# Wide and narrow products in turn: a tuned float32 trunk kernel with another order of its matmuls behind the mixer

## The chip, the cores and the metric

The kernel runs on one core of one Trainium2 chip. The metric is the device time of one execution in microseconds, lower being better. Profiles come from the hardware profiler; names such as L394 are lines of the kernel, PE is the matmul engine, DVE and ACT are the vector and the scalar engine, SP issues most of the transfers.

## The reference, cut to what matters

Two layers, each a token mixer and a gated feed-forward, run over 256 tokens of width 2048 in float32. Nearly all the work is products with large weights: `w_in` and `w_out` of both mixers, `w_up` (2048 by 11264) and `w_down` (5632 by 2048) of both feed-forwards.

```
for i in range(DEPTH):                      # DEPTH = 2
    h = rms_norm(x, mix_norm_w[i])
    x = x + (ssd_mixer(h, ...) if i == 0 else short_conv_mixer(h, ...))
    h = rms_norm(x, ffn_norm_w[i])
    x = x + conv_ffn(h, ffn_w_up[i], ffn_conv_w[i], ffn_conv_b[i], ffn_w_down[i])
return rms_norm(x, final_norm_w)

def short_conv_mixer(u, w_in, conv_w, w_out):
    bg, cg, h = jnp.split(u @ w_in, 3, axis=-1)
    return (bg * causal_dwconv(cg * h, conv_w)) @ w_out

def conv_ffn(u, w_up, conv_w, conv_b, w_down):
    hu = causal_dwconv(u @ w_up, conv_w, conv_b)
    g, v = jnp.split(hu, 2, axis=-1)
    return (jax.nn.silu(g) * v) @ w_down
```

## The kernel before, in words

Each float32 product is made of faster ones. A weight `w` is split on the chip into a rounded high part `wh` (a cast on ACT, L305) and the rest `wl` (a subtraction on DVE, L306); activations are kept as pairs of such parts side by side in one tile `hl`, 256 columns high part and 256 columns low part. Two products then do: a **wide** one, `wh` against all 512 columns, and a **narrow** one, `wl` against the 256 columns of the high part. A wide and a narrow product with the same block of weights are called a pair here.

Weights come in **units**: 256 rows by 512 columns, 512 KB, loaded by SP in the order of a plan, cast and split, with four buffers of `wh` and `wl`. A **stream** is one group of 512 output columns: it runs over all its units and sums into two PSUM tiles (`main`, made of two output blocks each). A unit holds two row blocks `k` and four column blocks `t`, so it gives eight pairs. A stream with 16 row blocks has 64 pairs, the down products of the first feed-forward have 24 row blocks in its first part (96 pairs) and 20 in the second (80 pairs).

Behind the first mixer all streams but those of the second down product go through `late_stream`. It works a unit in two halves of four pairs: half 0 fills the first PSUM tile, half 1, one unit behind, the second. The order of the matmuls on PE is fixed by `follow`, which chains each matmul to the one before it; the scheduler places everything else (DVE, ACT, small matmuls of a norm, recorded at L211 and L204, and the transposes at L906) by its own estimate of times. What `size` says sets the order inside a half: `size` wide products, then the `size` narrow ones of the same blocks.

- `size` 1 (streams with 16 row blocks): wide, narrow, wide, narrow.
- `size` 2 (the down streams): two wide, two narrow. "Two and two" below.
- `size` 4: in every stream, for the last two halves of the second PSUM tile. "Four and four" below.

The streams in order, with names that the text uses: the first feed-forward has part 1 (6 chunks, for each a gate stream and a value stream, then 4 down streams) and part 2 (5 chunks, then 4 down streams); then the second mixer, 12 streams `in` and 4 streams `out`; then the second feed-forward, part 1 (6 chunks) and part 2 (5 chunks), whose down products use another loop (L946 to L948, three wide products each).

When a PSUM tile is complete, `evac` reads it: ACT copies the columns 256 to 511 (L412), DVE adds the others (L414) and scales, convolves and gates.

Of the kernel before, what the change touches and what calls it, by code (L numbers as in the profile page):

```python
# [16 lines left out]
P = 128  # L17
T = 256
D = 2048
NKD = D // P  # L20
# [10 lines left out]
DFF = 5632  # L31
EPS = 1e-5
KU = 2
COLS = 512
WB = 4
FPARTS = ((0, 24), (24, 44))
ALL_COLS = tuple((cg, 0, DFF // P) for cg in range(D // COLS))
# [4 lines left out]
def trunk_kernel(ctx, tc, a, out):  # L42
# [20 lines left out]
    def follow(inst):  # L63

        if last_main[0] is not None:
            tc.add_manual_dep(
                inst.ins, last_main[0],
                mybir.DependencyInfo(
                    mybir.DependencyClass.NoSync, mybir.DependencyReason.DATA
                ),  # L70
                reason="stream order",
            )
        last_main[0] = inst.ins.name
        return inst
# [3 lines left out]
    def uid(s):  # L78
        n_id[0] += 1
        return f"{s}_{n_id[0]}"  # L80
# [61 lines left out]
    for name, r in rows:  # L142
        base[name] = at
        lo = 0
        while lo < r.shape[0]:
            i, off = divmod(at, P)
            n = min(P - off, r.shape[0] - lo)
# [72 lines left out]
    def rep2(t):  # L220
        return t.unsqueeze(1).to_broadcast([P, 2, T])

    def new_hl(pool=None):
        return (pool or hlpool).tile([P, 2, 2 * T], F32R, tag="hl", name=uid("hl"))
# [91 lines left out]
    def weight_unit(c0, kc, ahead=WB - 1):  # L316

        i = taken[0]
        assert plan[i][1:] == (c0, kc), (plan[i], c0, kc)
        taken[0] += 1  # L320
        while len(units) < min(i + ahead + 1, len(plan)):
            load_unit()
        got, units[i] = units[i], None
        return got
# [46 lines left out]
        for p in range(2):  # L371
            evac(p, pts[p])

    def late_stream(c0, hls, kcs, evac):


        pts = [psm.tile([P, 2, 512], F32, tag="main", name=uid("main")) for _ in range(2)]
        n = len(kcs)
        held = {}

        def half(p, u):
            wh, wl = held[u]
            blocks = [(t, k) for t in (2 * p, 2 * p + 1) for k in range(KU)]
            if p == 1 and u + 2 * KU >= n:
                size = len(blocks)
            else:
                size = 1 if n == NKD else KU
            for b in range(0, len(blocks), size):
                for w in (wh, wl):
                    for t, k in blocks[b : b + size]:  # L390
                        i = u + k
                        hl = hls[i // 2][:, i % 2, :]
                        cols = slice(0, 2 * T if w is wh else T)
                        follow(mm(  # L394
                            pts[p][:, t % 2, cols], w[:, k, t * P : (t + 1) * P], hl[:, cols],
                            start=(i == 0 and w is wh), stop=(i == n - 1 and w is wl),
                        ))

        for u in range(0, n + KU, KU):
            if u < n:  # L400
                held[u] = weight_unit(c0, kcs[u], WB - 2)
                half(0, u)
            if u:
                half(1, u - KU)
            while len(units) < min(taken[0] + WB - 1, len(plan)):
                load_unit()
        for p in range(2):
            evac(p, pts[p])
# [60 lines left out]
    xp, xhl = [], []  # L469
# [294 lines left out]
            hls.append(h)  # L764
        return hls

    def residual_stream(hls, kcs, norm, nhl, nname, put=stream, parts=ALL_COLS):

        if norm is not None:
            nhl += [None] * (NKD // 2)
        left = {cg: len(kcs) for cg, _, _ in parts}
        for cg, lo, hi in parts:
            hi = min(hi, len(kcs))
            left[cg] -= hi - lo

            def evac(p, pt, cg=cg, final=(left[cg] == 0)):
                m = 2 * cg + p  # L780
                x = xp[m]
                tt(out=x, in0=pt[:, :, 0:T], in1=x, op=ALU.add)
                tt(out=x, in0=pt[:, :, T : 2 * T], in1=x, op=ALU.add)
                if norm is not None and final:
                    norm.add(x)
                    h = new_hl()
                    split_pair(h, x, *nname(m))
                    nhl[m] = h

            put(cg * COLS, hls[lo // 2 : hi // 2], kcs[lo:hi], evac)  # L790

    yhl = []
    norm = Norm()
    nhl = []
# [33 lines left out]
    def ffn_part(l, part, hls, r):  # L828
        lo, hi = FPARTS[part]
        res = []  # L830
        for ch in range(lo, hi, 4):
            gs = []

            def evac_g(p, pt, ch=ch):
                k0 = ch + 2 * p
                y = conv(scaled(pt, r), W_FF, f"fw{l}", NF, k0, f"fb{l}", "g", gpool)
                act(y, y, AF.Silu)
                gs.append(y)

            def evac_v(p, pt, ch=ch):  # L840
                k0 = DFF // P + ch + 2 * p
                y = conv(scaled(pt, r), W_FF, f"fw{l}", NF, k0, f"fb{l}")
                tt(out=y, in0=gs[p], in1=y, op=ALU.mult)
                h = new_hl(hlpool2 if len(res) < 4 else hlpool)
                split_pair(h, y)
                res.append(h)

            late_stream(ch * P, hls, range(NKD), evac_g)
            late_stream(DFF + ch * P, hls, range(NKD), evac_v)
        return res  # L850

    xhl, nhl = nhl, []
    r = norm.row()
    norm = Norm()
# [9 lines left out]
    xhl, nhl = nhl, []  # L864
    r = norm.row()
    norm = Norm()
# [3 lines left out]
    for i in range(D // COLS):  # L870
        vs = [None, None]

        def evac_c(p, pt):
            s = pair_sum(pt)
            tt(out=s, in0=s, in1=rep2(r2), op=ALU.mult)
            vs[p] = s

        def evac_h(p, pt):
            s = pair_sum(pt)
            tt(out=s, in0=s, in1=vs[p], op=ALU.mult)  # L880
            vs[p] = conv(s, W_SC, "scw", NKD, 4 * i + 2 * p)

        def evac_b(p, pt):
            s = scaled(pt, r)
            tt(out=s, in0=s, in1=vs[p], op=ALU.mult)
            h = new_hl()
            split_pair(h, s)
            yhl.append(h)

        for n, ev in ((1, evac_c), (2, evac_h), (0, evac_b)):  # L890
            late_stream(n * D + i * COLS, xhl, range(NKD), ev)
    residual_stream(
        yhl, range(NKD), norm, nhl, lambda m: ("ffn", NKD + 2 * m), late_stream
    )
# [2 lines left out]
    xhl = nhl  # L897
# [30 lines left out]
    for part in range(2):  # L928
        lo, hi = FPARTS[part]
        hid = ffn_part(1, part, xhl, r)  # L930
        n = hi - lo
        for cg in range(D // COLS):
# [17 lines left out]
            def evac(c):  # L950
                x = xtok[c][:, cols]
                tt(out=x, in0=pt[:, c, :], in1=x, op=ALU.add)  # L952
                if part == 1:
                    junk = tmp.tile([P, 512], F32, tag="tp", name=uid("tp"))
                    act(junk, x, AF.Square, accum_out=ss[:, c, cg : cg + 1])
                    tt(out=x, in0=x, in1=fin[:, cols], op=ALU.mult)
                if end:
                    finish(c)
# [42 lines left out]
```

## Time and profile before

| what | value |
| --- | --- |
| median of 3 runs | 2541.95 us (2540.92 to 2543.9) |
| profiled execution, its time | 2543.58 us |
| its span, first to last instruction | 2541.7 us |
| PE busy | 2521.4 us (99%) |
| PE weight loads (beside PE's products) | 2194.3 us (86%) |
| DVE busy | 1782.5 us (70%) |
| ACT busy | 1356.2 us (53%) |
| transfers | 478.65 MB, mean 188 GB/s |
| granted TensorE clock | 0.999 |

A matmul's row in a timeline gives the start and a modelled duration. Durations overlap, since products are pipelined, so the pace is read from start to start. `x4` in such a row means four equal instructions in a run, merged into one line.

### The profile page before, as it was taken

What the parts mean: (1) busy time and instruction counts of PE and PEld (TensorE: products, weight loads), DVE (VectorE), ACT (ScalarE), POOL (GpSimd) and SP (SyncE); (2) the same over time, 40 slices, a digit from 0 to 9 for tenths busy, and PEclk for the clock granted to TensorE, in tenths of its full rate; (3) what the DMA queues carried; (4) which work ended last, traced back from release to release, by engine and by line L of the source; (5) the groups of instructions that cost most, each with busy time, mean ns of one, the idle gap of its engine ahead of it and who ended that gap; (6) DMA issues with size and microseconds to landing.
All of it is one profiled execution on the core that took longest, in us unless ns stands there. A gap on an engine that the chain in (4) does not pass through costs nothing.

```text
span 2541.7 us, 36880 instructions
## 1 busy us (share of the span) xinstructions
PE 2521.4 (99%) x14397; PEld 2194.3 (86%) x14397; DVE 1782.5 (70%) x2467; ACT 1356.2 (53%) x1738; POOL 1.1 (0%) x8
## 2 busy tenths in 40 slices
PE   9999999999999999999999999999999999999998
PEld 8888888888888888888888888888888888888886
DVE  7788875788777776557776666666677764577764
ACT  5676654566555554345554444444555553455543
POOL 0000000000000000000000000000000000000000
PEclk9999999999999999999999999999999999999999
DMA  7566656665666666666666666666566666666664
GB/s 229 176 192 197 190 179 190 190 174 177 200 182 191 191 190 187 188 190 190 191 191 187 186 190 190 189 189 193 174 188 189 189 198 191 190 185 190 190 198 141
DMA packets 255728, 478.65 MB, mean 188 GB/s; under 512 B 17667, under 2 KB 29123, under 8 KB 255427
## 3 DMA queue, kind: packets, MB, share of 16 engines
q1 hardware_dynamic: 254643, 474.13, 62.0%
q8 instruction: 112, 1.84, 0.3%
q10 hardware_dynamic: 912, 2.18, 0.2%
q14 instruction: 61, 0.50, 0.1%
HBM read 474.09 MB, written 2.16 MB: 187 GB/s over the span
## 4 chain that ended last, share of the span: by engine, by line
PE 98%; DMA 1%; DVE 1%; ACT 0%; issue 0%; SPq 0%; ACTq 0%; DVEq 0%
PE main L394 62%; PE main L360 15%; PE main L343 8%; PE main L946 3%; PE main L947 3%; PE main L948 3%; PE aux L725 1%; DMA raw<-in_ssd_w_in_dram 1%; DMA cbc<-cs_d 0%; PE aux L733 0%; PE aux L706 0%; PE aux L579 0%; PE aux L204 0%; PE main L358 0%; DVE wl L306 0%
## 5 line engine op out<-in xcount | busy, mean ns | idle before, releaser
L306 DVE TENSOR_TENSOR wl<-raw,wh 128x1024 fp32r<-128x1024 f32 (+1 forms) x881 | 1076.0, 1222 | 703.2 <-ACT wh L305 691.9
L394 PE MATMUL main<-hl,wh 128*128 128x512 f32 x4544 | 1516.0, 392 | 0.0
L305 ACT CAST wh<-raw 128x1024 fp32r<-128x1024 f32 (+1 forms) x881 | 924.6, 1050 | 1063.8 <-PE main L394 604.8
L394 PE MATMUL main<-hl,wl 128*128 128x256 f32 x4544 | 1154.2, 280 | 0.0
L394 PEld LDWEIGHTS main<-hl,wh 128*128 128x128 f32 x4544 | 818.7, 187 | 151.0
L394 PEld LDWEIGHTS main<-hl,wl 128*128 128x128 f32 x4544 | 838.6, 189 | 39.6
L360 PE MATMUL main<-hl,wh 128*128 128x512 f32 x1728 | 542.5, 397 | 1.4 <-DVE tp L420 1.3
L343 PEld LDWEIGHTS main<-hl,wl 128*128 128x128 f32 x1792 | 331.4, 188 | 76.2 <-DVE wl L306 3.5
L343 PE MATMUL main<-hl,wl 128*128 128x256 f32 x1792 | 359.2, 280 | 2.2 <-DVE wl L306 2.2
L360 PEld LDWEIGHTS main<-hl,wh 128*128 128x128 f32 x1728 | 266.5, 189 | 8.1 <-issue 4.9
L946 PE MATMUL main<-wh,hl 128*128 128x512 f32 x352 | 137.4, 390 | 0.8 <-DVE xtok L952 0.8
L947 PE MATMUL main<-wl,hl 128*128 128x512 f32 x352 | 137.5, 391 | 0.0
L948 PE MATMUL main<-wh,hl 128*128 128x512 f32 x352 | 137.0, 389 | 0.0
L412 ACT COPY tp<-main 128x512 f32<-128x512 f32 x150 | 86.7, 578 | 31.3 <-PE main L394 24.5
L414 DVE TENSOR_TENSOR tp<-main,tp 128x512 f32<-128x512 f32 x150 | 102.5, 683 | 0.6 <-ACT tp L412 0.6
L436 DVE SCALAR_TENSOR_TENSOR tp<-tp,prm,tp 128x255 f32<-128x255 f32 x208 | 90.3, 477 | 0.0
L423 DVE TENSOR_TENSOR tp<-tp,rrow 128x512 f32<-128x512 f32 x118 | 81.2, 688 | 1.9
L946 PEld LDWEIGHTS main<-wh,hl 128*128 128x128 f32 x352 | 66.1, 188 | 15.4 <-DVE xtok L952 1.2
L948 PEld LDWEIGHTS main<-wh,hl 128*128 128x128 f32 x352 | 66.1, 188 | 14.0
L947 PEld LDWEIGHTS main<-wl,hl 128*128 128x128 f32 x352 | 66.1, 188 | 13.6
L436 DVE SCALAR_TENSOR_TENSOR g<-tp,prm,g 128x254 f32<-128x254 f32 (+1 forms) x176 | 75.0, 477 | 1.2 <-ACT g L434 1.2
L434 ACT ACTIVATE tp<-tp,prm,prm 128x256 f32<-128x256 f32 x88 | 48.0, 593 | 1.6 <-DVE tp L423 1.6
(140 smaller groups left out, 1011.7 us busy)
## 6 DMA issues: line engine op xcount, KB each, us to landing
raw<-in_ffn_w_up_dram SPq DMA_DIRECT2D x352, 512.0 KB, 4.0
raw<-in_ffn_w_down_dram SPq DMA_DIRECT2D x176, 512.0 KB, 3.7
raw<-in_ssd_w_in_dram SPq DMA_DIRECT2D x159, 512.0 KB, 4.7
raw<-in_sc_w_in_dram SPq DMA_DIRECT2D x96, 512.0 KB, 3.8
raw<-in_ssd_w_out_dram SPq DMA_DIRECT2D x64, 512.0 KB, 3.8
raw<-in_sc_w_out_dram SPq DMA_DIRECT2D x32, 512.0 KB, 3.7
cbc<-cs_d SPq DMA_DIRECT2D x32, 256.0 KB, 5.8
xt<-in_x_dram SPq DMA_DIRECT2D x8, 256.0 KB, 6.8
```

Of the source, the lines that this page charges most:

```text
L305: put(nc.scalar.copy(wh[:, ks, :], raw[:, ks, :]))
L306: put(tt(out=wl[:, ks, :], in0=raw[:, ks, :], in1=wh[:, ks, :].bitcast(F32), op=ALU.subtract,))
L343: put(mm(pts[t // 2][:, t % 2, 0:T], wl[:, k, t * P : (t + 1) * P], hls[i // 2][:, i % 2, 0:T], start=False, stop=(i == n - 1),))
L360: put(mm(o, wh[:, k, lw], hl, start=first, stop=False))
L394: follow(mm(pts[p][:, t % 2, cols], w[:, k, t * P : (t + 1) * P], hl[:, cols], start=(i == 0 and w is wh), stop=(i == n - 1 and w is wl),))
L412: nc.scalar.copy(pb, pt[:, :, T : 2 * T])
L414: tt(out=s, in0=pt[:, :, 0:T], in1=pb, op=ALU.add)
L423: tt(out=s, in0=s, in1=rep2(r), op=ALU.mult)
L436: stt(out=y[:, j, d:T], in0=s[:, j, 0 : T - d], scalar=pcol(wname, (width - 1 - d) * nk + k0 + j), in1=y[:, j, d:T], op0=ALU.mult, op1=ALU ...
L946: follow(mm(pt[:, c, :], hi_, wh[:, k, :], start=(i == 0), stop=False))
L947: follow(mm(pt[:, c, :], hi_, wl[:, k, :], start=False, stop=False))
L948: follow(mm(pt[:, c, :], lo_, wh[:, k, :], start=False, stop=(i == n - 1)))
```

## The change

In `late_stream`, `size` is now 1 everywhere, also in the down streams and in the last halves of a stream. Only where a stream is called with `settle=True` does it run two and two, and its last two halves of the second PSUM tile four and four. Settled are:

- the first gate stream of each part of both feed-forwards (`ch == lo`),
- the first value stream of the second feed-forward (`ch == 0 and l == 1`),
- the first `in` stream of the second mixer (`i == 0 and n == 1`),
- the last column block of the first feed-forward's down product, in each part (2 streams).

That is six streams with 16 row blocks, which were alternating before, and two down streams, which stay as they were.

```
-            if p == 1 and u + 2 * KU >= n:
-                size = len(blocks)
-            else:
-                size = 1 if n == NKD else KU
+            size = 1
+            if settle:
+                size = len(blocks) if p == 1 and u + 2 * KU >= n else KU
...
-            put(cg * COLS, hls[lo // 2 : hi // 2], kcs[lo:hi], evac)
+            if put is late_stream and len(kcs) != NKD and cg == D // COLS - 1:
+                kw = {"settle": True}
+            put(cg * COLS, hls[lo // 2 : hi // 2], kcs[lo:hi], evac, **kw)
...
-            late_stream(ch * P, hls, range(NKD), evac_g)
-            late_stream(DFF + ch * P, hls, range(NKD), evac_v)
+            late_stream(ch * P, hls, range(NKD), evac_g, ch == lo)
+            late_stream(DFF + ch * P, hls, range(NKD), evac_v, ch == 0 and l == 1)
...
-            late_stream(n * D + i * COLS, xhl, range(NKD), ev)
+            late_stream(n * D + i * COLS, xhl, range(NKD), ev, i == 0 and n == 1)
```

No instruction is added or taken away on any engine. SP and POOL keep their order row for row; PE, DVE and ACT change theirs from the first feed-forward on. The built programs show it at three places; line numbers of the changed kernel are three to five higher (L397 is the old L394).

On PE, the end of the first gate stream of the first feed-forward (a settled one) and the start of the next. `main_7101` and `main_7102` are its PSUM tiles, `main_7305` the next stream's first. Before:

```order
L204 MATMUL aux_7095<-dg_7092,ones 128x128 x2
L394 MATMUL main_7101<-hl_7056,wh_7201 128x512
L394 MATMUL main_7101<-hl_7056,wl_7202 128x256
L394 MATMUL main_7101<-hl_7056,wh_7201 128x512
L394 MATMUL main_7101<-hl_7056,wl_7202 128x256
L394 MATMUL main_7102<-hl_7046,wh_7179 128x512 x4
L394 MATMUL main_7102<-hl_7046,wl_7180 128x256 x4
L394 MATMUL main_7102<-hl_7056,wh_7201 128x512 x4
L394 MATMUL main_7102<-hl_7056,wl_7202 128x256 x4
L394 MATMUL main_7305<-hl_6848,wh_7223 128x512
L394 MATMUL main_7305<-hl_6848,wl_7224 128x256
```

The same place in the changed kernel:

```order
L397 MATMUL main_7101<-hl_7056,wh_7201 128x512 x2
L397 MATMUL main_7101<-hl_7056,wl_7202 128x256 x2
L397 MATMUL main_7101<-hl_7056,wh_7201 128x512
L204 MATMUL aux_7095<-dg_7092,ones 128x128 x2
L397 MATMUL main_7101<-hl_7056,wh_7201 128x512
L397 MATMUL main_7101<-hl_7056,wl_7202 128x256 x2
L397 MATMUL main_7102<-hl_7046,wh_7179 128x512 x4
L397 MATMUL main_7102<-hl_7046,wl_7180 128x256 x4
L397 MATMUL main_7102<-hl_7056,wh_7201 128x512 x4
L397 MATMUL main_7102<-hl_7056,wl_7202 128x256 x4
L397 MATMUL main_7305<-hl_6848,wh_7223 128x512
L397 MATMUL main_7305<-hl_6848,wl_7224 128x256
```

The body went from alternating to two and two, the end stays four and four, and the norm's small matmuls (L204) moved by one product.

On PE, the end of the next stream, the first value stream (`main_7305`, `main_7306`), and the start of the one behind it (`main_7515`). Before:

```order
L394 MATMUL main_7305<-hl_7056,wl_7406 128x256
L394 MATMUL main_7306<-hl_7046,wh_7383 128x512 x4
L394 MATMUL main_7306<-hl_7046,wl_7384 128x256 x4
L394 MATMUL main_7306<-hl_7056,wh_7405 128x512 x4
L394 MATMUL main_7306<-hl_7056,wl_7406 128x256 x4
L394 MATMUL main_7515<-hl_6848,wh_7427 128x512
L394 MATMUL main_7515<-hl_6848,wl_7428 128x256
```

In the changed kernel:

```order
L397 MATMUL main_7306<-hl_7056,wh_7405 128x512
L397 MATMUL main_7306<-hl_7056,wl_7406 128x256
L397 MATMUL main_7515<-hl_6848,wh_7427 128x512
L397 MATMUL main_7515<-hl_6848,wl_7428 128x256
L397 MATMUL main_7515<-hl_6848,wh_7427 128x512
```

The four and four at the end is gone: the products alternate through the end of the stream and into the next.

On DVE, the eviction of that value stream (`main_7306`) among the splits of the next weights. Before:

```order
L306 TENSOR_TENSOR wl_7472<-raw_7469,wh_7471 128x1024
L306 TENSOR_TENSOR wl_7528<-raw_7525,wh_7527 128x1024
L436 SCALAR_TENSOR_TENSOR tp_7488<-tp_7485,prm_127,tp_7488 128x255 x2
L414 TENSOR_TENSOR tp_7501<-main_7306,tp_7499 128x512
L436 SCALAR_TENSOR_TENSOR tp_7488<-tp_7485,prm_126,tp_7488 128x254 x2
L423 TENSOR_TENSOR tp_7501<-tp_7501,rrow_7098 128x512
```

In the changed kernel (L439, L417, L426 and L848 are the old L436, L414, L423 and L843):

```order
L306 TENSOR_TENSOR wl_7472<-raw_7469,wh_7471 128x1024
L439 SCALAR_TENSOR_TENSOR tp_7488<-tp_7485,prm_127,tp_7488 128x255 x2
L439 SCALAR_TENSOR_TENSOR tp_7488<-tp_7485,prm_126,tp_7488 128x254 x2
L306 TENSOR_TENSOR wl_7528<-raw_7525,wh_7527 128x1024
L417 TENSOR_TENSOR tp_7501<-main_7306,tp_7499 128x512
L848 TENSOR_TENSOR tp_7488<-g_7284,tp_7488 128x512
L426 TENSOR_TENSOR tp_7501<-tp_7501,rrow_7098 128x512
```

One split (`wl_7528`) moved behind four passes of the convolution; ACT moves the cast that belongs to it behind two activations.

More of the change, by code (lines that the diff above doesn't have):

```diff
@@ L372, in stream, with late_stream @@
             evac(p, pts[p])
-    def late_stream(c0, hls, kcs, evac):
+    def late_stream(c0, hls, kcs, evac, settle=False):
         pts = [psm.tile([P, 2, 512], F32, tag="main", name=uid("main")) for _ in range(2)]
@@ L765, in ssd_gate, with residual_stream @@
         return hls
-    def residual_stream(hls, kcs, norm, nhl, nname, put=stream, parts=ALL_COLS):
+    def residual_stream(hls, kcs, norm, nhl, nname, put=stream, parts=ALL_COLS, **kw):
         if norm is not None:
```

## Prediction

> **What bounds the kernel now.** First the page: busy times, the chain that ended last, the costliest groups.
>
> ```profile
> PE 2521.4 (99%) x14397; PEld 2194.3 (86%) x14397; DVE 1782.5 (70%) x2467; ACT 1356.2 (53%) x1738; POOL 1.1 (0%) x8
> ...
> PE 98%; DMA 1%; DVE 1%; ACT 0%; issue 0%; SPq 0%; ACTq 0%; DVEq 0%
> ...
> L306 DVE TENSOR_TENSOR wl<-raw,wh 128x1024 fp32r<-128x1024 f32 (+1 forms) x881 | 1076.0, 1222 | 703.2 <-ACT wh L305 691.9
> L394 PE MATMUL main<-hl,wh 128*128 128x512 f32 x4544 | 1516.0, 392 | 0.0
> L305 ACT CAST wh<-raw 128x1024 fp32r<-128x1024 f32 (+1 forms) x881 | 924.6, 1050 | 1063.8 <-PE main L394 604.8
> L394 PE MATMUL main<-hl,wl 128*128 128x256 f32 x4544 | 1154.2, 280 | 0.0
> ```
>
> PE carries 98% of the chain, and behind the 4544 wide and 4544 narrow products of `late_stream` stands no idle time at all. So a reordering can only act through the pace from one product's start to the next, or by making PE wait where it doesn't now. Second, who waits for whom, over all engines:
>
> ```profile
> DVE wl L306 <- ACT wh L305: 691.9, 540, 4.1
> ACT wh L305 <- PE main L394: 604.8, 493, 3.5
> ```
>
> The columns are total us, times, longest. DVE waits for casts, and casts wait for PE to give up a weight buffer: the supply of weights runs as far ahead as four buffers let it. PE is the bound, not DVE (70%), ACT (53%) or the transfers.
>
> Third, the timeline of PE, for the pace. A value stream in part 2 of the first feed-forward, up to its end:
>
> ```profile
> 1172.16 0.40 PE L394 MATMUL main<-hl,wh 128*128 128x512 f32 x1
> ...
> 1172.86 0.39 PE L394 MATMUL main<-hl,wh 128*128 128x512 f32 x1
> 1173.09 0.28 PE L394 MATMUL main<-hl,wl 128*128 128x256 f32 x1
> ...
> 1190.54 0.39 PE L394 MATMUL main<-hl,wh 128*128 128x512 f32 x1
> ...
> 1191.58 1.09 PE L394 MATMUL main<-hl,wh 128*128 128x512 f32 x4
> 1192.50 0.64 PE L394 MATMUL main<-hl,wl 128*128 128x256 f32 x4
> 1192.98 1.09 PE L394 MATMUL main<-hl,wh 128*128 128x512 f32 x4
> 1193.91 0.63 PE L394 MATMUL main<-hl,wl 128*128 128x256 f32 x4
> 1194.38 0.40 PE L394 MATMUL main<-hl,wh 128*128 128x512 f32 x1
> ```
>
> Between the wide products at 1172.86 and 1190.54 lie 51 alternating pairs: 17.68 us, **346.7 ns a pair**. The eight pairs done four and four take 1191.58 to 1194.38, 2.80 us, **350 ns a pair**. Two and two, in the second down stream of part 1 (20 groups of two pairs):
>
> ```profile
> 1021.22 0.63 PE L394 MATMUL main<-hl,wh 128*128 128x512 f32 x2
> ...
> 1035.15 0.63 PE L394 MATMUL main<-hl,wh 128*128 128x512 f32 x2
> ```
>
> 13.93 us over 40 pairs: **348.2 ns**. But alternating has a second pace. The last part of the second feed-forward begins behind the other loop's products:
>
> ```profile
> 2197.69 0.39 PE L948 MATMUL main<-wh,hl 128*128 128x512 f32 x1
> 2197.91 0.39 PE L394 MATMUL main<-hl,wh 128*128 128x512 f32 x1
> ...
> 2198.97 0.40 PE L394 MATMUL main<-hl,wh 128*128 128x512 f32 x1
> ...
> 2216.99 0.40 PE L394 MATMUL main<-hl,wh 128*128 128x512 f32 x1
> ```
>
> 2198.97 to 2216.99 is again 51 pairs, 18.02 us: **353.3 ns**. Same instructions, same clock, 6.6 ns a pair slower, and it holds for a whole stream and the next. The instructions of L394 by stretch tell the two apart by the middle one of the three wide durations (least, median, most), 391 ns fast and 398 ns slow:
>
> ```profile
> L394 PE MATMUL main<-hl,wh x640: 387/391/398, 727.4 to 948.8; 128*128 128x512 f32 x160
> ...
> L394 PE MATMUL main<-hl,wh x128: 389/398/403, 2197.9 to 2242.4; 128*128 128x512 f32 x128
> ...
> L394 PE MATMUL main<-hl,wh x64: 389/398/477, 703.9 to 726.6; 128*128 128x512 f32 x64
> ...
> L394 PE MATMUL main<-hl,wh x65: 389/396/476, 1819.1 to 1844.7; 128*128 128x512 f32 x65
> ...
> L394 PE MATMUL main<-hl,wh x64: 387/391/397, 1439.1 to 1461.6; 128*128 128x512 f32 x64
> ```
>
> Ten streams from 727.4 are fast; slow are the first gate stream (703.9, behind the mixer's loop), the first value stream of the second feed-forward (1819.1, most of it, with transposes between) and the two at 2197.9. So the pace depends on what stood ahead, it persists, and the four and four at a stream's end is where it turns from slow to fast (727.4, 2243) or doesn't (between the two at the end).
>
> Last, the lengths of whole streams, from the first wide product of one to that of the next (columns: stretch, length, PE, weight loads, DVE, ACT, POOL, clock, transfers):
>
> ```profile
> 1172.16:1194.38 22.22, 22.22 (x130) 19.57 (x129) 15.34 (x21) 12.63 (x17) 0.00 (x0) 1.00 0.66 190
> 1005.20:1038.64 33.44, 33.44 (x195) 29.24 (x194) 17.10 (x17) 12.61 (x13) 0.00 (x0) 1.00 0.62 189
> 1355.56:1383.42 27.86, 27.86 (x162) 24.37 (x161) 16.83 (x20) 13.15 (x17) 0.00 (x0) 1.00 0.62 189
> 2197.91:2220.49 22.58, 22.58 (x129) 19.60 (x128) 11.56 (x12) 9.27 (x10) 0.00 (x0) 1.00 0.60 170
> 2220.49:2243.07 22.58, 22.58 (x130) 19.62 (x129) 15.35 (x21) 12.62 (x17) 0.00 (x0) 1.00 0.62 186
> 703.89:727.35 23.46, 23.46 (x138) 20.52 (x137) 17.69 (x35) 12.35 (x17) 0.00 (x0) 1.00 0.59 168
> 1439.14:1462.29 23.15, 23.15 (x138) 20.48 (x137) 17.71 (x35) 11.93 (x17) 0.00 (x0) 1.00 0.60 183
> 1819.14:1844.69 25.55, 25.55 (x158) 22.59 (x157) 15.36 (x21) 15.54 (x23) 0.00 (x0) 1.00 0.53 155
> ```
>
> **The change part by part.** A fully alternating stream of 16 row blocks at the fast pace takes 64 x 346.7 = 22.19 us; of 24 row blocks 96 x 346.7 = 33.28, of 20 row blocks 27.73. A settled stream of 16 takes 56 x 348.2 + 8 x 350 = 22.30.
>
> 1. Four and four taken out of streams that alternate. Behind the mixer stand 60 streams of 16 row blocks; 6 are settled, one more (2220.49) was slow, 53 remain: 22.22 - 22.19 = 0.033 us each, unrounded. Gain 1.75 us.
> 2. The stream at 2220.49, no longer behind a slow one: 22.58 - 22.19. Gain 0.39 us.
> 3. Down streams, three in each part, from two and two to alternating: 3 x (33.44 - 33.28) + 3 x (27.86 - 27.73). Gain 0.87 us.
> 4. The six settled ones. The norm's small products cost 23.15 - 22.22 = 0.93 us in a stream. First gate stream: 22.30 + 0.93 = 23.23 for 23.46, gain 0.23. Part 2 of the first feed-forward, the second mixer's first stream and the first gate stream of the second feed-forward were fast: a loss of 0.08 each, 0.24. The value stream at 1819.14 was slow for more than half its 64 pairs, 32 to 64 x 6.6 ns = 0.2 to 0.4, less 0.08: gain 0.1 to 0.3, taken as 0.15. The stream at 2197.91: 22.58 - 22.30 = 0.28. Together a gain of 0.42.
> 5. What the scheduler moved. DVE is busy for at most 17.7 of 23 us in any of the streams above, so the split that goes behind four passes has 5 us of slack a stream; the norm's products come, by the built order, twelve products (some 2 us) earlier in one stream and later in another. Taken as nothing: DVE's idle time and the buffers ahead cover it. If that cover were gone, the next half of PE would start late, by about the 1050 ns of one cast (L305).
> 6. Buffers and PSUM tiles of a stream's end are given up later, by three narrow products: at 0.64 us for four (the row at 1192.50) less than 0.5 us, behind the same cover.
>
> Sum 1.75 + 0.39 + 0.87 + 0.42 = **3.4 us** gained, against the profiled execution's span of 2541.7: 2538.3. That execution took 2543.58 us, 1.63 above the median of 2541.95, so the forecast in the metric is 2541.95 - 3.4 = **2538.6 us**.
>
> All this holds only if alternation runs at the fast pace. Before, it was set anew at the end of each stream; now it runs on from a settled stream to the next settled one, in five stretches: 11 streams and 3 down streams (992 pairs), 9 and 3 (816), 15 of the second mixer (960), 10 (640) and 9 (576). The price of a slow stretch is its pairs times 6.6 ns: 6.6, 5.4, 6.4, 4.3 and 3.8 us, 26 us for all. What the trace has of the way into a stretch: two and two all through, then four and four, then alternating, as here behind the last down stream of part 1:
>
> ```profile
> 1104.10 1.09 PE L394 MATMUL main<-hl,wh 128*128 128x512 f32 x4
> 1105.03 0.63 PE L394 MATMUL main<-hl,wl 128*128 128x256 f32 x4
> 1105.50 0.40 PE L394 MATMUL main<-hl,wh 128*128 128x512 f32 x1
> ...
> 1106.55 0.39 PE L394 MATMUL main<-hl,wh 128*128 128x512 f32 x1
> ```
>
> Three pairs in 1.05 us, fast. The stream at 1439.1 (391 ns) entered in the same way. Two of two, but both behind down streams without a small matmul inside. Behind the mixer's two and two without a four and four, alternation was slow (703.9). I take the fast pace for each stretch, by the two nearest rows, with doubt for each; the second stretch most, whose first stream is now settled directly behind another settled one, which no row shows. How alternation goes over the down streams' own activation tiles no row shows either: between 346.7 and 353.3 ns.
>
> **The rivals.**
> - One stretch falls into the slow pace and keeps it: 2538.6 + 3.8 to 6.6 = 2542.4 to 2545.2; with the second, 2544.0. For it: the slow pace went through one stream's end into the next at 2220.49. Against: of the four slow streams three ended fast, and all streams begun fast and left undisturbed stayed so; but there are no such ends now to mend a slow one.
> - Two or more stretches slow, the case on the other side: from 2538.6 + 3.8 + 4.3 = 2546.7 up to 2565 with all five. It decides from about 1300 slow pairs (8.5 us, by which the gain is lost and 0.2% more).
> - The order makes no difference, so that nothing is gained: 2542. Four paces for the same work in the rows above speak against it. The Trainium skill (TensorE: Matmul & The Clock Gate, section "Back-to-back issue gap") gives a product alone N / 2.4 + 2.5 ns; as an estimate that is 215.8 + 109.2 = 325 ns a pair in any order. By that rule the sum is zero; the trace does not agree, with 346.7 to 353.3 by order and history.
> - Late weights: a cast or split comes late in each of the 54 alternating streams. At 1050 ns each that is 57 us; the waits above speak against it.
>
> **How the numbers follow.** This measurement tells about 0.2%, 5.1 us, from no change. Fast throughout 47%, 2537.5 to 2539.5; one slow stretch 30%; two or more 13%; no difference 4%; late weights 2%; a gain past 5.1 us, by a pace that no row shows or in the measurement, 4%. The first, second and fourth lie within 0.2% but for a little noise: faster 5%, same 80%, slower 15%. The range takes in the fast case with its noise and one slow stretch: 2536.5 to 2546.5.
>
> **What the profile after would show.** PE's groups of `late_stream` still without idle time; streams of 22.19 us, the down streams 33.28 and 27.73 but for the last, 22.3 for settled ones, and a median wide duration of 391 ns in all five stretches. A stretch of 22.6 us streams with 398 ns would show the first rival, waits of PE for L306's successor the last. What makes me wrong is mainly a state that I can read but not derive.

## The result, and the profile after

The changed kernel takes 2548.95 us (median of 9 runs, 2547.67 to 2551.55), the one before 2541.95 (median of 9, 2539.42 to 2543.9): a ratio of 1.003, with a 95% interval of 1.0021 to 1.0039. It is slower by 7 us, where the forecast said faster by 3.4 and allowed up to 2546.5. The profiled execution took 2551.55 us, with a span of 2549.3, which is 7.6 above the span before.

First the page of the changed kernel: busy times, chain, costliest groups (L397 is the old L394).

```profile
PE 2529.3 (99%) x14397; PEld 2196.0 (86%) x14397; DVE 1789.4 (70%) x2467; ACT 1355.7 (53%) x1738; POOL 1.1 (0%) x8
...
PE 98%; DMA 1%; DVE 1%; ACT 0%; issue 0%; SPq 0%; DVEq 0%; ACTq 0%
...
L306 DVE TENSOR_TENSOR wl<-raw,wh 128x1024 fp32r<-128x1024 f32 (+1 forms) x881 | 1075.6, 1222 | 700.4 <-ACT wh L305 692.2
L397 PE MATMUL main<-hl,wh 128*128 128x512 f32 x4544 | 1566.2, 394 | 0.0
L305 ACT CAST wh<-raw 128x1024 fp32r<-128x1024 f32 (+1 forms) x881 | 923.8, 1049 | 1053.9 <-PE main L397 638.5
L397 PE MATMUL main<-hl,wl 128*128 128x256 f32 x4544 | 1225.8, 280 | 0.0
```

PE is the bound as before, and behind its products of `late_stream` still stands no idle time (the last column is 0.0). The two groups of products show 1566 and 1226 us of busy time, more than before, but these sums overlap and are not lengths. Who waits for whom, over all engines (total us, times, longest):

```profile
DVE wl L306 <- ACT wh L305: 692.2, 584, 4.1
ACT wh L305 <- PE main L397: 638.5, 466, 3.4
```

Casts wait for PE 34 us longer in all: the supply of weights has more slack, not less. So nothing came late. The loss is in PE's pace, and the windows show where. Each row is one stretch between two first wide products, with the late products alone (columns: window, length, PE, weight loads, clock, transfers). The rows are the 11 up streams of stretch 1, its three alternating down streams, the 9 up streams of stretch 2, its three down streams, the 15 of the second mixer, the first 9 of stretch 4, the first 8 of stretch 5. Before:

```profile
727.35:971.77 244.42, 244.42 (x1410) 215.27 (x1409) 1.00 0.64 189
971.77:1072.07 100.30, 100.30 (x579) 87.69 (x577) 1.00 0.61 189
1127.72:1327.70 199.98, 199.98 (x1154) 176.13 (x1153) 1.00 0.65 190
1327.70:1411.28 83.58, 83.58 (x482) 73.10 (x481) 1.00 0.62 189
1462.30:1795.60 333.30, 333.30 (x1923) 293.55 (x1922) 1.00 0.63 189
1844.69:2044.67 199.98, 199.98 (x1154) 176.13 (x1153) 1.00 0.65 190
2220.49:2398.61 178.12, 178.12 (x1026) 156.62 (x1025) 1.00 0.64 189
```

After:

```profile
726.68:970.74 244.06, 244.06 (x1410) 215.19 (x1409) 1.00 0.64 189
970.74:1072.40 101.66, 101.66 (x579) 88.27 (x578) 1.00 0.61 187
1128.15:1331.67 203.52, 203.52 (x1154) 176.59 (x1153) 1.00 0.64 187
1331.67:1416.33 84.66, 84.66 (x482) 73.57 (x481) 1.00 0.61 186
1467.42:1800.22 332.80, 332.80 (x1922) 293.43 (x1921) 1.00 0.63 189
1849.32:2052.84 203.52, 203.52 (x1155) 176.40 (x1153) 1.00 0.64 186
2228.75:2406.25 177.50, 177.50 (x1027) 156.50 (x1025) 1.00 0.65 190
```

Stretches 1, 3 and 5 gained 0.36, 0.50 and 0.62 us. Stretches 2 and 4 lost 3.54 each (some 3.9 with the tenth stream of stretch 4), and the two groups of down streams lost 1.36 and 1.08. In stretch 2 every stream takes 203.52 / 9 = 22.61 us, 353.3 ns a pair: the slow pace that the prediction had read, kept for nine streams. The late products' wide durations (least, median, most) in that stretch say the same, 398 in the middle:

```profile
L397 PE MATMUL main<-hl,wh x576: 395/398/403, 1128.2 to 1331.3; 128*128 128x512 f32 x192
```

Two places are to be explained: how a stretch gets its pace, and why the down streams have the slow one though stretch 1 ran into them at the fast one. First the way into stretch 1 (fast) and into stretch 2 (slow), from PE's timeline (start, modelled duration, run length at the end of the row). Both come out of a settled gate stream through the same two halves of four and four; the one into stretch 1 has the norm's small products three products ahead of them.

```profile
723.90 1.08 PE L397 MATMUL main<-hl,wh 128*128 128x512 f32 x4
724.81 0.64 PE L397 MATMUL main<-hl,wl 128*128 128x256 f32 x4
725.28 1.09 PE L397 MATMUL main<-hl,wh 128*128 128x512 f32 x4
726.22 0.63 PE L397 MATMUL main<-hl,wl 128*128 128x256 f32 x4
726.68 0.40 PE L397 MATMUL main<-hl,wh 128*128 128x512 f32 x1
...
727.73 0.39 PE L397 MATMUL main<-hl,wh 128*128 128x512 f32 x1
```

```profile
1125.34 1.09 PE L397 MATMUL main<-hl,wh 128*128 128x512 f32 x4
1126.27 0.63 PE L397 MATMUL main<-hl,wl 128*128 128x256 f32 x4
1126.74 1.09 PE L397 MATMUL main<-hl,wh 128*128 128x512 f32 x4
1127.67 0.64 PE L397 MATMUL main<-hl,wl 128*128 128x256 f32 x4
1128.15 0.40 PE L397 MATMUL main<-hl,wh 128*128 128x512 f32 x1
...
1129.21 0.40 PE L397 MATMUL main<-hl,wh 128*128 128x512 f32 x1
```

The first four wide products take 723.90 to 724.81, 0.91 us, in the one and 0.93 in the other; behind them three pairs take 1.05 and 1.06 us. Unrounded, the gaps from each start to the next show more (ns, worked out from the trace's start times; W wide, n narrow, "small" the norm's products):

```
two and two, all through:  W 233 236  n 116 112 (A)   W 233 230  n 114 119 (B)   A   B   A ...

into stretch 1 (fast):     small, 3 products | W 235 227 226 227  n 113 120 120 120 (Q) | W 233 236 228 233  n 117 119 118 116 (P) | W 235 n 117  W 230 n 117
into stretch 2 (slow):     ... A B | W 233 236 228 233  n 117 120 117 117 (P) | W 235 233 236 224  n 118 120 120 120 (Q) | W 233 n 117  W 241 n 120
before, at 1104.10 (fast): ... B A | W 232 231 227 226  n 114 119 120 120 (Q) | W 233 236 228 233  n 117 120 117 117 (P) | W 235 n 116  W 230 n 117
before, at 1439.1 (fast):  ... B A | W 233 231 226 227  n 113 119 120 120 (Q) | W 234 236 228 232  n 118 119 118 116 (P) | W 235 n 117  W 230 n 117
```

Two and two has two kinds of group, A and B, that follow each other strictly. A half of four and four has two forms as well: P, and Q, whose last three narrow gaps are 119 or 120. A half behind B takes form P, one behind A form Q, and of two in a row the second takes the other form. (A half right behind small products can have a third form, as in pad below.) Alternation behind P is fast, behind Q slow. So the pace of a stretch hangs on where in a rhythm of two its four and four begins, and on how many halves of it there are. Behind the small products the rhythm starts anew. In the kernel before, this reading fits all 57 places where a four and four led into plain alternation: 56 behind P are fast, the one behind Q (at 2220.49) is slow.

### The profile page after: what moved, and what is told of

It is laid out like the page before. It is cut to its first block, busy times and chain, and to the rows that moved or that the text cites. A ratio compares the mean times of both kernels' runs of the same rounds, so it can differ in the third digit from the quotient of the medians.

```text
span 2549.3 us, 36886 instructions
## 1 busy us (share of the span) xinstructions
PE 2529.3 (99%) x14397; PEld 2196.0 (86%) x14397; DVE 1789.4 (70%) x2467; ACT 1355.7 (53%) x1738; POOL 1.1 (0%) x8
## 4 chain that ended last, share of the span: by engine, by line
PE 98%; DMA 1%; DVE 1%; ACT 0%; issue 0%; SPq 0%; DVEq 0%; ACTq 0%
PE main L397 62%; PE main L360 15%; PE main L343 8%; PE main L951 3%; PE main L952 3%; PE main L953 3%; PE aux L728 1%; DMA cbc<-cs_d 0%; PE aux L736 0%; PE aux L709 0%; PE aux L582 0%; DMA raw<-in_ssd_w_in_dram 0%; PE aux L204 0%; PE main L358 0%; DVE wl L306 0%
## 5 line engine op out<-in xcount | busy, mean ns | idle before, releaser
L397 PE MATMUL main<-hl,wh 128*128 128x512 f32 x4544 | 1566.2, 394 | 0.0
L397 PE MATMUL main<-hl,wl 128*128 128x256 f32 x4544 | 1225.8, 280 | 0.0
L397 PEld LDWEIGHTS main<-hl,wh 128*128 128x128 f32 x4544 | 833.1, 188 | 174.8
L397 PEld LDWEIGHTS main<-hl,wl 128*128 128x128 f32 x4544 | 855.5, 189 | 23.0
L360 PE MATMUL main<-hl,wh 128*128 128x512 f32 x1728 | 542.4, 397 | 1.3 <-DVE tp L423 1.3
L343 PEld LDWEIGHTS main<-hl,wl 128*128 128x128 f32 x1792 | 332.0, 188 | 75.3 <-DVE wl L306 2.5
L343 PE MATMUL main<-hl,wl 128*128 128x256 f32 x1792 | 359.7, 281 | 1.6 <-DVE wl L306 1.6
L360 PEld LDWEIGHTS main<-hl,wh 128*128 128x128 f32 x1728 | 266.5, 189 | 7.8 <-issue 4.9
L417 DVE TENSOR_TENSOR tp<-main,tp 128x512 f32<-128x512 f32 x150 | 102.4, 683 | 1.6 <-ACT tp L415 1.6
L439 DVE SCALAR_TENSOR_TENSOR tp<-tp,prm,tp 128x255 f32<-128x255 f32 x208 | 88.6, 477 | 0.0
L426 DVE TENSOR_TENSOR tp<-tp,rrow 128x512 f32<-128x512 f32 x118 | 81.2, 688 | 2.5
L439 DVE SCALAR_TENSOR_TENSOR g<-tp,prm,g 128x254 f32<-128x254 f32 (+1 forms) x176 | 73.5, 478 | 1.2 <-ACT g L437 1.2
```

Source lines behind the costliest of these rows:

```text
L343: put(mm(pts[t // 2][:, t % 2, 0:T], wl[:, k, t * P : (t + 1) * P], hls[i // 2][:, i % 2, 0:T], start=False, stop=(i == n - 1),))
L360: put(mm(o, wh[:, k, lw], hl, start=first, stop=False))
L397: follow(mm(pts[p][:, t % 2, cols], w[:, k, t * P : (t + 1) * P], hl[:, cols], start=(i == 0 and w is wh), stop=(i == n - 1 and w is wl),))
L417: tt(out=s, in0=pt[:, :, 0:T], in1=pb, op=ALU.add)
L426: tt(out=s, in0=s, in1=rep2(r), op=ALU.mult)
L439: stt(out=y[:, j, d:T], in0=s[:, j, 0 : T - d], scalar=pcol(wname, (width - 1 - d) * nk + k0 + j), in1=y[:, j, d:T], op0=ALU.mult, op1=ALU ...
```

## What was tested

The theory on history: the pace comes from the rhythm ahead, so one half of four and four less (or more) at a settled stream's end swaps the pace of the stretch behind it, whichever it is. Its rival, on place: a stretch is slow for something of its own (its tiles, its buffers). On the down streams: their first four activation tiles come from the pool `hlpool2`, which by the addresses of the built program begins 64 bytes past a multiple of 128 bytes, while all other activation tiles and the weights begin on multiples of 512. The flip stands right at their start (PE's timeline of the changed kernel, wide products at the entry of the first down stream, rows between left out):

```profile
970.74 0.39 PE L397 MATMUL main<-hl,wh 128*128 128x512 f32 x1
...
971.44 0.40 PE L397 MATMUL main<-hl,wh 128*128 128x512 f32 x1
...
972.85 0.40 PE L397 MATMUL main<-hl,wh 128*128 128x512 f32 x1
```

Two pairs take 0.70 us, the next four 1.41 (352.5 ns). Names of kernels stand in bold; where no interval is given, a kernel was run once, and the reading rests on its windows, not on its time. The windows and gaps of each kernel come from one profiled execution.

### One half of four and four instead of two

**one_end**, at every settled stream:

```
-                size = len(blocks) if p == 1 and u + 2 * KU >= n else KU
+                size = len(blocks) if p == 1 and u + KU >= n else KU
```

> Settled streams end with one four-and-four half instead of two; nothing else differs from the changed kernel. Theory (the pace of a stretch is set by where in the two-and-two rhythm the four and four begins): each extra four and four swaps the outcome, so stretches turn round. First-feed-forward part 2 and second-feed-forward part 1, slow in the changed kernel (22.61 us a stream), become fast (22.19); part 1 of the first and part 2 of the second, fast there, become slow (22.61); the second mixer is open, a norm's products stand right at its settled stream's end. Sum for the up streams: 11 x 0.42 - 9 x 0.42 - 10 x 0.42 + 9 x 0.42 = +0.4 us, +6.7 if the mixer turns slow. Rival (a stretch is slow because of its place: its weights, its tiles, its neighbours): the same stretches stay slow, time unchanged within 1 us.

2549.95 us, beside 2542.1 for the kernel before on the same chip. The windows of stretch 1, 2, 3 and 5:

```profile
724.94:973.69 248.75, 248.75 (x1411) 215.92 (x1409) 1.00 0.59 186
...
1131.07:1330.76 199.69, 199.69 (x1155) 176.43 (x1154) 1.00 0.60 190
1466.49:1799.30 332.81, 332.81 (x1923) 294.04 (x1922) 1.00 0.61 189
...
2223.50:2404.41 180.91, 180.91 (x1026) 157.18 (x1025) 1.00 0.59 186
```

Stretch 1 turned slow (22.61 a stream), stretch 2 fast (22.19), stretch 5 slow; stretch 4 turned fast as well (199.69 for its nine). The down streams did not move (101.66 and 84.67). Stretch 3 stayed fast. The gaps at the entries:

```
into stretch 1 (slow): ... A | W 233 230 227 227  n 113 119 120 120 (Q) | W 234 n 117  W 241 n 120
into stretch 2 (fast): ... B | W 233 237 227 233  n 117 120 117 117 (P) | W 235 n 116  W 230 n 117
into stretch 3 (fast): small | W 315 233  n 124 118 | W 232 231  n 113 119 (B) | W 234 236 228 232  n 118 120 117 116 (P) | W 235 n 117  W 231 n 116
```

The form of the last half decides: one Q leaves alternation slow, one P leaves it fast. Stretch 3 has no swap because in the changed kernel its small products stand right ahead of the first half (which took form Q and was followed by P), and here between them and the half lie two groups, so that the half falls behind a B. The rival on place falls: the same stretches, tiles and buffers ran at the other pace.

### One half where two end slow

**parity** keeps two halves and takes one only at the first gate stream of part 2 of the first feed-forward and at the first value stream of the second feed-forward, the ones ahead of stretches 2 and 4:

```
-                size = len(blocks) if p == 1 and u + 2 * KU >= n else KU
+                size = len(blocks) if p == 1 and u + settle * KU >= n else KU
...
-                kw = {"settle": True}
+                kw = {"settle": 2}
...
-            late_stream(ch * P, hls, range(NKD), evac_g, ch == lo)
+            late_stream(ch * P, hls, range(NKD), evac_g, (ch == lo) * (1 if part and not l else 2))
...
-            late_stream(n * D + i * COLS, xhl, range(NKD), ev, i == 0 and n == 1)
+            late_stream(n * D + i * COLS, xhl, range(NKD), ev, 2 * (i == 0 and n == 1))
```

> As the changed kernel, but one four-and-four half instead of two only in the settled streams ahead of the two slow stretches (first gate stream of part 2 of the first feed-forward, first value stream of the second feed-forward). Theory of the rhythm: both stretches run at 22.19 us a stream instead of 22.61: 9 x 0.42 + 10 x 0.42 = 8.0 us less than the changed kernel, about 2541. The down streams stay at 33.88 and 28.2. Rival of the place: no change, about 2549. Rival of chance (the pace falls differently from build to build): one of the two fast, or another stretch slow.

2541.01 us (median of 10), ratio to before 0.9998 (0.9988 to 1.0007): 7.9 us under the changed kernel's median. Stretch 2, then the three down streams of part 1:

```profile
1126.41:1326.09 199.68, 199.68 (x1154) 176.41 (x1153) 1.00 0.59 189
...
969.01:1070.66 101.65, 101.65 (x578) 88.41 (x577) 1.00 0.57 187
```

All five stretches of up streams are fast now, stretch 4 with 199.69, each behind a half of form P; the down streams still run at 33.88 and 28.23. Two halves in the whole program were worth the 7 us that the change had lost.

### Four and four back at every end

**ends** keeps the settled streams and gives every alternating stream its two halves of four and four back:

```
-            size = 1
+            size = len(blocks) if p == 1 and u + 2 * KU >= n else 1
```

> As the changed kernel, but every alternating stream again ends with two four-and-four halves, the down streams too. Theory (the ends were what turned a slow pace fast before): the first stream of each slow stretch still takes about 22.6 us, then the stretch is fast at 22.22; down streams stay near 33.9, their pace is set by something else. 8 x 0.39 + 9 x 0.39 = 6.6 us less, 1 us more for the ends themselves: 5 to 6 us below the changed kernel. Rival (the ends do nothing for the pace): slow stretches stay at 22.6 and the time rises by about 1 us.

2542.82 us beside 2542.1 before. Stretch 2:

```profile
1125.74:1326.08 200.34, 200.34 (x1154) 176.17 (x1153) 1.00 0.60 189
```

That is 22.58 for the first stream and 22.22 for the eight others: the first enters slow, its own end mends it, and the rest pay 0.033 us each for that. So before, the four and four at each end was what kept a slow entry down to one stream, or to two (the slow pace passed the end ahead of 2220.49). Its cost was 1.75 us in all, and with these ends back the changed kernel took some 6 us less (2548.95 less 2542.82, the latter a single run).

### The activation tiles of the down streams

**pad** is the changed kernel with a 64-byte tile placed ahead, so that `hlpool2` begins on a multiple of 512:

```
+    fill = small.tile([P, 16], F32, tag="fill", name="fill", bufs=1)
+    nc.vector.memset(fill, 0.0)
```

> As the changed kernel, with 64 unused bytes a partition ahead of the pool of the first four activation tiles of a down product, so that these tiles start on a multiple of 512 bytes as all others do (in the changed kernel: 64 bytes past a multiple of 128). Theory (alternating over tiles at that offset runs slow and leaves the slow pace behind): the three alternating down streams of part 1 go from 33.88 to about 33.28 us, 1.8 us less; in part 2 they follow the pace of their stretch; the two settled down streams lose 0.05 us each, and since their rhythm begins otherwise, the stretches behind them may turn (part 2 fast: 5 us less; second mixer slow: 6 us more). Rival (down streams alternate slowly for another reason, such as their 24 row blocks): 33.88 as it was.

2553.52 us (median of 4), ratio 1.005 (1.0035 to 1.0065). The down streams of part 1, and the second mixer:

```profile
968.60:1068.44 99.84, 99.84 (x578) 88.03 (x577) 1.00 0.58 190
...
1463.63:1802.83 339.20, 339.20 (x1922) 294.21 (x1921) 1.00 0.60 186
```

The down streams fell from 33.88 to 33.28 us, which is the forecast's figure to the hundredth, so the place of the tiles was what made them slow. But the kernel got slower: stretches 2 and 4 stay slow, so the down streams of part 2 entered slow and stay so (28.27), and the second mixer, fast in the changed kernel, is now slow (22.61 a stream, 6.4 us): its small products stand behind a group A instead of B, the half right behind them has a third form (W 315 229 233 236  n 112 117 118 120), and its last half has form Q.

**best_a** joins parity and pad.

> The one-half ends ahead of the two slow stretches and the 64 unused bytes together. Theory (the rhythm sets the pace of a stretch, the tiles' offset that of the down streams): the two stretches and all six alternating down streams fast, 33.28 and 27.73. Open is the second mixer, slow with the 64 bytes alone: its settled stream is entered from a down stream whose pace is another one now. Mixer fast: the sum of the forecast holds with the fast pace everywhere, 3.4 us below the kernel before, 2538.6. Mixer slow: 15 x 0.42 = 6.3 us more, 2544.9.

2543.65 us, ratio 1.0009 (1.0000 to 1.0018). The down streams are fast in both parts (33.28 and 27.73), stretches 1, 2, 4 and 5 too, and the second mixer is slow with the same 339.20 as in pad. **best_b** is best_a with one half instead of two at the second mixer's settled stream (its call as in the changed kernel, `i == 0 and n == 1`, which counts as 1).

> As the kernel with one-half ends and the 64 bytes, and the second mixer's settled stream ends with one four-and-four half too. Theory of the rhythm: its 15 alternating streams run at the pace that they do not have with two halves, so one of the two kernels is at 2538.6 and the other at 2544.9. Rival (with a norm's products next to the end, one or two halves make no difference there): both alike.

2537.49 us (median of 10), ratio 0.9981 (0.9972 to 0.9990). The down streams of part 1 and the second mixer:

```profile
969.56:1069.40 99.84, 99.84 (x579) 88.03 (x578) 1.00 0.58 191
...
1459.15:1791.95 332.80, 332.80 (x1922) 293.43 (x1921) 1.00 0.60 189
```

Now every alternating stream is fast, and the time comes within 1.1 us of the forecast's 2538.6: 2542.16 before on the same chip less 2537.49 is 4.7 us, where the sum had 3.4.

### Where the offset acts

Is it the place of the activations, that of the weights, or the distance between them? **hl_off** is parity with 64-byte gaps around `hlpool`, so that all activation tiles of the late streams lie 64 past a multiple of 128 and the weights don't:

```
+    gap0 = ctx.enter_context(tc.tile_pool(name="gap0", bufs=1)).tile([P, 16], F32, tag="gap0", name="gap0")
+    nc.vector.memset(gap0, 0.0)
     hlpool = ctx.enter_context(tc.tile_pool(name="hlpool", bufs=16))
+    gap1 = ...                               # the same again
```

> As the kernel with one-half ends, but with all activation tiles hl moved to 64 bytes past a multiple of 128 (64 unused bytes ahead of their pool and behind it; weights stay on multiples of 128). Theory (the offset of the activation tiles decides): alternating runs at 353 ns a pair in every stream, 53 x 0.42 = 22 us more, while two and two runs at 346.7 instead of 348.2, 2.6 us less over the first mixer's 1728 pairs: 2541 + 22 - 3 = 2560. Rival (only those four tiles, or the down streams, are special): 2541, alternating streams at 22.19.

**w_off** has such gaps around `wpool` instead: the weights lie at 64, the activations of the streams with 16 row blocks on multiples of 128.

> As the kernel with one-half ends (alternating, activation tiles on multiples of 512 bytes), but the weight tiles wh and wl at 64 bytes past a multiple of 128. Theory 1 (only the offset of the activation tiles counts): streams 22.19, as without it, about 2541. Theory 2 (the difference between the two operands' offsets counts): alternating streams at 22.6, as with the activation tiles moved, about 2562.

2562.33 and 2562.04 us, 20.2 and 21.5 us over the kernel before on their chips. Stretch 1 and the second mixer of hl_off, then of w_off:

```profile
721.75:970.48 248.73, 248.73 (x1410) 216.12 (x1409) 1.00 0.59 186
1466.89:1806.08 339.19, 339.19 (x1922) 294.66 (x1921) 1.00 0.59 186
```

```profile
722.42:971.16 248.74, 248.74 (x1411) 216.05 (x1409) 1.00 0.63 186
1467.40:1806.59 339.19, 339.19 (x1922) 294.65 (x1921) 1.00 0.61 186
```

Every alternating stream of 16 row blocks takes 22.61 us in both, in all ten stretches: where the two operands lie 64 bytes apart modulo 128, alternation showed the slow pace alone, and which of the two was moved makes no difference. The settled streams went the other way: without small products inside they took 22.19 to 22.20 instead of 22.29 to 22.33. Unrounded, their two and two has one kind of group only (W 226 236  n 118 114, to 1 or 2 ns), where the aligned tiles gave A and B in turn: there is no rhythm of two left to begin at the wrong place.

That points to another version: two and two everywhere, with the operands 64 bytes apart. **all22_off** is that, and **all22** the same order with the tiles of the changed kernel:

```
-            size = 1
-            if settle:
-                size = len(blocks) if p == 1 and u + 2 * KU >= n else KU
+            size = KU
```

> Two and two everywhere, no four and four, no alternating, and all activation tiles at 64 bytes past a multiple of 128. Theory of the offset: 346.7 ns a pair in every stream, the mixer too, with no state to fall into: streams 22.19, down streams 33.28 and 27.73; against the kernel before 2.0 us for 60 streams' ends, 1.2 for its slow streams, 1.1 for its down streams, 2.6 for its first mixer, 2535. Rival (two and two is 348.2 on these tiles wherever they lie): 22.29 a stream, about 2545.

> Two and two everywhere as in the fastest kernel so far, but with the activation tiles back on multiples of 512 bytes. Theory of the offset: 348.2 ns a pair, 22.29 a stream; the first four tiles of a down product lie at the odd offset as before, so down streams 33.4 and 27.8; first mixer as in the kernel before. 64 x 1.5 ns more for each of 60 streams, about 6 us, and 2.6 of the mixer: 8 to 9 us above the kernel with the offset, about 2544. Rival (taking out four and four was what helped, not the offset): about 2535.

all22_off took 2535.37 us (median of 7), ratio 0.9973 (0.9962 to 0.9984), the fastest of all here; all22 took 2545.51, beside 2540.54 before. Stretch 1 of each, all22_off first:

```profile
720.67:964.73 244.06, 244.06 (x1411) 214.35 (x1410) 1.00 0.60 189
```

```profile
725.90:971.13 245.23, 245.23 (x1410) 214.06 (x1409) 1.00 0.64 189
```

22.19 us a stream with the offset and 22.29 without it: with the offset two and two has the pace of fast alternation, and no entry decides over it. Most of its gain lies elsewhere: its first late product starts at 697.6 us, in the kernel before at 703.89. From there to the end its profiled execution took 1835.6 us, 2.2 less than before (1837.8), while best_b took 1833.6. The first mixer's loop ahead reads the same moved tiles, but with unmoved activation tiles the first late product also came as early as 699.85 (best_a); how much the offset brings there isn't shown. So its time on the forecast's 2535 is in part luck.

Last, **both_off**: best_b's ends, with activations and weights all at 64 past a multiple of 128, so that they lie no distance apart.

> As the kernel with one-half ends in all three places and aligned tiles, but with activation tiles and weight tiles both at 64 bytes past a multiple of 128, so that between them the offset is zero. Theory 2 (the difference counts): alternating streams at 22.19, down streams at 33.28 and 27.73, as with both on multiples of 512, 2537.5, unless a stretch turns. Rival (any operand off a multiple of 128 slows alternating): streams at 22.6, about 2562.

2547.26 us (median of 10), ratio 1.0023 (1.0013 to 1.0032). The down streams of part 1, stretch 2, the second mixer and stretch 4:

```profile
967.83:1067.67 99.84, 99.84 (x579) 88.03 (x577) 1.00 0.61 190
1123.44:1323.12 199.68, 199.68 (x1154) 176.06 (x1153) 1.00 0.65 190
1457.41:1796.62 339.21, 339.21 (x1923) 294.11 (x1921) 1.00 0.61 186
1845.62:2049.14 203.52, 203.52 (x1154) 176.55 (x1153) 1.00 0.64 186
```

The fast pace is back, in the down streams and in stretches 1, 2 and 5, which hl_off and w_off had not: it is the distance that counts. But the second mixer and stretch 4 are slow, which best_b with the same order of PE's products had fast. The gaps in the second mixer's settled stream:

```
best_b:   ... B A | small | W 314 229  n 117 118 | W 233 230  n 114 119 (B) | W 233 236 228 233  n 117 120 117 117 (P) | fast
both_off: ... B A | small | W 313 224  n 118 120 | W 233 236  n 116 112 (A) | W 233 231 226 227  n 113 119 120 120 (Q) | slow
```

Ahead of the small products both stand alike but for the very last gap (113 ns in best_b, 119 in both_off), behind them the rhythm starts on the other group. So the order alone doesn't set where it starts again. What does wasn't isolated, and stays open: it may be the moment at which the small products are released, or the place of their own tiles (by the addresses of the built programs, the tile `dg` that they read lies on a multiple of 128 bytes in best_b and 64 past one in both_off). What holds in each of the 35 entries into stretches of these seven kernels (after, one_end, parity, pad, best_a, best_b, both_off) is the rest: behind P fast, behind Q slow.

## Why the prediction was wrong, by its steps

**The step that failed** is "I take the fast pace for each stretch, by the two nearest rows". Both rows showed a four and four that began behind an A; nothing in them said so, since rows rounded to 10 ns don't show A and B apart. The prediction had named stretch 2 as the doubtful one, for its first stream settled "directly behind another settled one", and there it did fall: the first gate stream's four and four began behind a B. So did that of the value stream ahead of stretch 4. Naming stretch 2 was luck, though: the streams ahead of stretches 3 and 4 are also settled directly behind a settled one, stretch 3 was fast, and one_end ran stretch 2 fast behind the same streams. The rival of two or more slow stretches came true, which had 13%; in hindsight it deserved about as much as the fast case, as five entries stood on a state of two values that two rows had sampled on one side. A second step failed beside it, term 3 of the sum, the down streams (item 3 below). The 19 slow streams of stretches 2 and 4 cost 8.0 us against the forecast, the down streams 3.3.

**The price was right.** Stretches 2 and 4 and the three down streams of part 1 make 816 + 640 + 288 = 1744 slow pairs at 6.6 ns, 11.5 us. On the forecast's span of 2538.3 that is 2549.8; the profile has 2549.3.

1. Four and four taken out: 0.033 us a stream was forecast. Stretch 3 gained 0.50 in 15 streams, stretch 1 0.36 in 11. Right, wherever the pace was fast.
2. The stream behind the slow one: stretch 5's eight streams gained 0.62, which is 0.39 and seven times 0.033. Right.
3. Down streams: forecast a gain of 0.87, measured a loss of 1.36 + 1.08 = 2.4. The second unknown, how alternation goes over the down streams' own tiles, was left between 346.7 and 353.3 ns and taken at the fast end without a reason. With the slow end it would have been 96 x 353.3 = 33.9 a stream, which came. pad shows the cause in part 1, the tiles' place; in part 2 either cause would have done it alone: the slow entry (28.27 in pad, with the tiles aligned) or the tiles' place (28.23 in parity, entered fast).
4. Settled streams: forecast 0.42. The first gate stream (703.50 to 726.68) took 23.19 for 23.23; the stream ahead of stretch 5 22.29 for 22.30; part 2's and the second mixer's first streams lost 0.11 and 0.07 for 0.08 each; the first two streams of the second feed-forward together took the same to 0.01, where 0.07 less was forecast. In all some 0.38. Right.
5. and 6. The scheduler's moves and the later buffers cost nothing: no idle time behind L397, and casts that wait longer for PE than before. Right.

That the order would make no difference (4%) is refuted by the windows of stretches 2 and 4 (22.61 us a stream for 22.22 before); late weights came nowhere.

## What to carry to other kernels

Here the matmul engine waited for nothing, and a stretch of equal products could still have two lengths, and the profile shows which by the length of one stream. So read several streams, and at each change of order read the gaps ahead of it unrounded, not only the order. A gain that rests on such a state needs either something that sets it again at short intervals (the four and four cost 1.75 us, and with them the changed kernel took some 6 less) or an order and placement that showed no second state (two and two with operands 64 bytes apart, 22.19 us a stream). And a tile moved by 64 bytes is a change of its own: compare kernels with the same addresses, or vary them on purpose.

## What the runs showed of the hardware

- The same 64 pairs of wide and narrow products, with no wait, took 22.19 or 22.61 us when alternating, and a stretch kept its pace over 15 streams (332.80 or 339.20 for the second mixer). Which one can be read in the last four pairs of four and four ahead of the change of order: fast behind form P, slow behind form Q, in 35 of 35 entries with the operands 0 apart modulo 128.
- The distance of the two operands' places modulo 128 bytes decides which paces there are. At 0: alternating 346.7 or 353.3 ns a pair, two and two 348.3 (22.29 / 64). At 64: alternating 353.3 only, two and two 346.7. Other distances weren't tried, and it isn't shown what makes the rhythm.
- The Trainium skill (TensorE: Matmul & The Clock Gate, section "Back-to-back issue gap") gives, at one state of the clock, a gap by the number of columns alone. The windows here don't agree with that: at a granted clock of 1.00 they differ by 1.9% for the same columns, by order, place and history (22.19 and 22.61 us).
